# An S5 layer in split fp32 on one core: high and low parts a step apart, table work spread, one chain for two rows of x, and all residuals added from SBUF

## The chip, the cores and the metric

One core of a Trainium2 chip runs the whole program. Its engines are named as in the profile: PE (TensorE, matmuls; PEld is its weight load), DVE (VectorE), ACT (ScalarE), POOL (GpSimd) and SP (SyncE); SP and POOL also issue DMAs, each in its own order, one queue per engine. The metric is the device time of one execution in microseconds; a lower one is better. Times of a run are given as the median of several executions.

## The reference

The model is a trunk of interleaved mixers, but with depth 1 only layer 0 runs, which is the S5 state-space layer. x has 1024 positions of 2048 features:

```
h    = RMSNorm(x) * pre_norm
u, z = split(h @ w_in)                       # 2048 x 4096
A    = exp((a_re + i a_im) dt), dt = exp(log_dt)          # 128 groups x 64 states
B    = (A - 1)/(a_re + i a_im) * (b_re + i b_im)          # 16 channels to 64 states, each group
st_t = A st_(t-1) + B u_t                    # over 1024 positions
y    = Re(C st) + d_skip * u
g    = gelu(y)
y    = g * sigmoid(g @ w_glu + b_glu) * silu(z)           # 2048 x 2048
out  = x + RMSNorm(y @ w_out) * post_norm                 # 2048 x 2048
```

## The kernel before

**Split products.** Every large product is made of three: each fp32 operand is split into a high part (a copy rounded to the matmul's format, by ACT) and a low part (the rest, operand minus high part, by DVE), and PE adds high x high, high x low and low x high into one PSUM bank. `split_piece` does this for a weight piece of 128x512: an ACT copy (L171) and a DVE subtraction (L176). Where a weight term is itself a difference that no earlier step has stored, a DVE subtraction (L168) comes first. `split` (L833, L834) does the same for activations.

**Positions.** Row s of the eight "rows" of x holds positions 8k+s; a half is four such rows. x's rows are loaded, squared (`sq_x`: ACT L268 for even column blocks, DVE L270 for odd ones), turned into a reciprocal root (`rstd_x`, `_rsqrt`) and a scaled identity (`diag_x`), and transposed by PE (`trans_x`, L297) into the activations `hT`. At the start rows 0 and 1 have one chain together, rows 2 and 3 one each.

**Stage 1, the input projection.** 32 column tiles of `w_in` (16 for u, 16 for z) in two halves, in `units`; each inner turn is one block of 128 rows (L911, L913, L915). A weight piece covers four turns and is loaded (`load_piece`, on SP) and split a few pieces ahead (`begin_piece`; LA pieces for the load, SA for the split). Background work is handed out by `advance`, once per turn and half; such a unit is called a slot. First runs the generator `prep`, one `yield` per slot: it transposes tables on PE (L493), negates and copies (DVE L503, L504, ACT L495), multiplies the B coefficients (DVE L516, L517, L519) and stores the tables to DRAM from POOL. Then `plan` puts S5's work into slots: 32 heads (four groups each), one every TICK = 26 slots, each with a list of steps at fixed offsets (`s5_steps`: loads, coefficients, rotation, a scan on DVE L685, products L641, L667, L699, L700, gelu). Offsets ahead of the start are clamped to start + 1. Sums and differences of weight blocks for the next stages (`weight_sums`, L739) come every TSET = 19 slots: loads, and six and eight slots later the subtractions.

**Stages 2 and 3, GLU and output product.** Both are one level of Strassen's scheme in Winograd's form: seven products of half-size blocks each (`GLU_ORDER`, `OUT_ORDER`; L1229). Each product takes 16 steps (two column halves of eight), a step being one weight piece and its twelve matmuls. After each step `step()` hands out other work from five queues under a budget of four DVE operations: `front` (PSUM evacuation), `back` (next product's activations, by `ahead`: load, and two items later use), `mid` (gates, sums), `gains` (multiplying by post_norm, L1126) and `side` (weight sums left over, later the finished rows). The last product of the output stage is finished one row at a time with all its weights in SBUF (L1246 to L1248).

**The residual.** During stage 1, 23 DMAs on SP copy x (256 KB each) straight from DRAM into the output. When rows are done, `out_scale_tile` scales a 128x512 tile on ACT (L1165) and POOL's queue adds it onto the output in DRAM (L1162). Nine of the 32 tiles go the other way: x is loaded to SBUF (L1172), DVE scales and adds (L1178), SP stores plainly (L1179).

**Order.** Instructions are issued in the program's order on each engine and each queue; a tile's buffer is reused when its last reader is done. Nothing is reordered by a scheduler. Three buffers hold high weight parts in stage 1, four later; seven and later nine hold raw weights and low parts.

## Time and profile before

| | |
|---|---|
| median of 3 runs | 1516.75 us (1516.06 to 1519.03) |
| the profiled execution | 1519.02 us, its span 1517.2 us |
| PE busy | 1474.1 us, 97% of the span, 7288 matmuls |
| DVE busy | 1101.6 us, 73%, 2158 instructions |
| ACT busy | 666.3 us, 44% |
| POOL busy | 406.8 us, 27% |
| DMA | 332.01 MB, mean 219 GB/s |
| granted PE clock | 0.994 of full over the execution |

A row of the profile has the line of the kernel, the engine, the operation, the tile written and the tiles read, then busy time; in a timeline the first two numbers are start and length in us, and what stands in square brackets is the engine's idle time before the instruction and what ended it. PE is given as busy almost throughout, but a matmul's modelled length (some 0.39 us for 512 columns) is longer than the distance from one start to the next, so counts of starts in a window tell more than busy time.

### The profile page before, as it was taken

How to read it: one execution, taken by the hardware profiler on the slowest of the kernel's cores; microseconds unless marked ns; L12 is line 12 of the kernel's file. 1: busy time of each engine (PE TensorE's matmuls, PEld its weight loads, DVE VectorE, ACT ScalarE, POOL GpSimd, SP SyncE). 2: the span in 40 equal slices, each digit the busy share in tenths (PEclk: the TensorE clock that was granted, in tenths of full speed). 3: DMA queues.
4: the chain of work that ended last, by engine and by line, in shares of the span. 5: the costliest groups of instructions: out<-in, count | busy, mean ns of one | idle time of the engine just before them, and what ended most of it. 6: DMA issues, size and time to landing. Idle time of an engine off the chain costs nothing.

```text
span 1517.2 us, 22596 instructions
## 1 busy us (share of the span) xinstructions
PE 1474.1 (97%) x7288; PEld 1195.8 (79%) x7288; DVE 1101.6 (73%) x2158; ACT 666.3 (44%) x1223; POOL 406.8 (27%) x730
## 2 busy tenths in 40 slices
PE   6989999999999999999999999999999999998996
PEld 6867887878888888888888888788888878886774
DVE  7774888888878889888876346765788763577756
ACT  6642344444545454454543343432344353333553
POOL 5912243433434333423332102100112310000031
PEclk9999999999999999999999999999999999999998
DMA  7376767768677767765564449995889984675587
GB/s 275 97 231 170 227 171 231 211 200 237 183 225 207 237 173 237 201 186 170 149 195 132 156 160 335 358 311 164 293 314 358 370 297 160 182 222 190 160 209 170
DMA packets 252183, 332.01 MB, mean 219 GB/s; under 512 B 31280, under 2 KB 150112, under 8 KB 250912
## 3 DMA queue, kind: packets, MB, share of 16 engines
q1 hardware_dynamic: 217536, 251.14, 53.0%
q0 software_dynamic: 34528, 79.43, 17.2%
q8 instruction: 57, 0.93, 0.3%
q14 instruction: 62, 0.51, 0.1%
HBM read 244.54 MB, written 91.82 MB: 222 GB/s over the span
## 4 chain that ended last, share of the span: by engine, by line
PE 82%; DMA 7%; DVE 5%; issue 2%; ACT 2%; SPq 1%; POOL 0%; DVEq 0%; ACTq 0%; POOLq 0%
PE ps_d L911 15%; PE ps_d L1229 15%; PE ps_d L913 15%; PE ps_d L915 15%; PE ps_s L1229 14%; PE ps_s L667 2%; PE ps_s L700 2%; PE ps_s L699 2%; DMA w_raw<-in_s_w_out_dram 2%; DMA w_raw<-glu_T 1%; DVE w_raw L176 1%; ACT w_hi L171 1%; PE ps_s L641 1%; DMA gl<-g_d 1%; PE ps_s L297 1%
## 5 line engine op out<-in xcount | busy, mean ns | idle before, releaser
L171 ACT ACTIVATE w_hi<-w_raw 128x512 fp32r<-128x512 f32 x320 | 200.6, 630 | 487.6 <-PE ps_d L913 254.0
L176 DVE TENSOR_TENSOR w_raw<-w_raw,w_hi 128x512 fp32r<-128x512 f32 x320 | 222.3, 697 | 220.7 <-ACT w_hi L171 214.9
L911 PE MATMUL ps_d<-act,w_hi 128*128 128x512 f32 x1024 | 335.7, 404 | 0.0
L913 PE MATMUL ps_d<-act,w_hi 128*128 128x512 f32 x1024 | 322.8, 391 | 0.0
L915 PE MATMUL ps_d<-act,w_raw 128*128 128x512 f32 x1024 | 321.9, 390 | 0.0
L915 PEld LDWEIGHTS ps_d<-act,w_raw 128*128 128x128 f32 x1024 | 192.8, 188 | 41.3
L913 PEld LDWEIGHTS ps_d<-act,w_hi 128*128 128x128 f32 x1024 | 192.9, 188 | 40.8 <-DVE act L304 0.7
L911 PEld LDWEIGHTS ps_d<-act,w_hi 128*128 128x128 f32 x1024 | 185.2, 189 | 43.5 <-issue 10.2
L1229 PE MATMUL ps_d<-w_hi,act 128*128 128x512 f32 x448 | 140.7, 392 | 0.6 <-ACT w_hi L171 0.6
L1229 PE MATMUL ps_d<-act,w_hi 128*128 128x512 f32 x448 | 139.5, 392 | 0.0
L1229 PE MATMUL ps_s<-act,w_hi 128*128 128x512 f32 x448 | 139.3, 392 | 0.0
L1229 PE MATMUL ps_s<-w_hi,act 128*128 128x512 f32 x384 | 121.7, 395 | 3.2 <-ACT w_hi L171 3.2
L717 POOL DMA_DIRECT2D g_d<-gel_g x128 | 77.6, 614 | 144.8 <-DVE gel_g L715 133.8
L654 POOL DMA_DIRECT2D T<-hp_d x128 | 76.8, 618 | 110.4 <-issue 69.7
L1229 PEld LDWEIGHTS ps_d<-w_hi,act 128*128 128x128 f32 x448 | 84.1, 188 | 19.9 <-ACT w_hi L171 1.5
L1229 PEld LDWEIGHTS ps_s<-act,w_hi 128*128 128x128 f32 x448 | 84.1, 188 | 19.1
L1229 PEld LDWEIGHTS ps_d<-act,w_hi 128*128 128x128 f32 x448 | 84.0, 188 | 19.2 <-DVE ev L858 0.3
L833 ACT ACTIVATE act<-act 128x512 fp32r<-128x512 f32 x112 | 69.8, 626 | 57.2 <-DVE act L1019 29.8
L739 DVE TENSOR_TENSOR wsum<-wsum 128x256 f32<-128x256 f32 x156 | 65.9, 422 | 37.7 <-DMA wsum<-in_s_w_glu_dram 21.0
L1229 PE MATMUL ps_d<-w_raw,act 128*128 128x512 f32 x224 | 88.7, 396 | 1.1 <-DVE w_raw L176 1.0
L1162 POOL DMA_DIRECT2D out_dram<-act x23 | 19.8, 924 | 259.9 <-ACT act L1165 259.9
L1229 PE MATMUL ps_d<-act,w_raw 128*128 128x512 f32 x224 | 88.2, 394 | 1.3 <-DVE w_raw L176 1.3
(289 smaller groups left out, 2372.0 us busy)
## 6 DMA issues: line engine op xcount, KB each, us to landing
w_raw<-in_s_w_in_dram SPq DMA_DIRECT2D x136, 256.0 KB
w_raw<-in_s_w_out_dram SPq DMA_DIRECT2D x80, 256.0 KB
act<-g_d SPq DMA_DIRECT2D x72, 256.0 KB
wsum<-in_s_w_glu_dram SPq DMA_DIRECT2D x128, 128.0 KB
glu_T<-wsum POOLq DMA_DIRECT2D x128, 128.0 KB, 5.2
w_raw<-glu_T SPq DMA_DIRECT2D x64, 256.0 KB
w_raw<-in_s_w_glu_dram SPq DMA_DIRECT2D x48, 256.0 KB
u_d<-ev SPq DMA_DIRECT2D x128, 64.0 KB
```

What stands on the lines that cost most here:

```text
L171: act.activation(h, lf, AF.Copy)
L176: v.tensor_tensor(l, lf, h.bitcast(F32), op=OP.subtract)
L654: nc.gpsimd.dma_start(t[:, g], bass.AP(tensor=a.tensor, offset=a.offset + 16, ap=[[16, 8], [256, 16], [1, 128]]))
L667: pe.matmul(pv[64 * par:64 * par + 64, hh, i], lhsT=st["W1"][:, 2 * i + par, hh], rhs=st["U"][:, 2 * i + par], start=True, stop=True, tile ...
L699: pe.matmul(py[:, g], lhsT=st["T"][:, g], rhs=st["U"][:, g], start=True, stop=False)
L717: nc.gpsimd.dma_start(g_d[blk][4 * o + j].rearrange("c s k -> s c k"), g[:, NK * j:NK * j + NK])
L739: v.tensor_tensor(b[into], b[x], b[y], op=OP.subtract)
L833: act.activation(h, r, AF.Copy)
L911: pe.matmul(o, lhsT=wh[:, js], rhs=xh, start=kt == 0, stop=False)
L913: pe.matmul(o, lhsT=wh[:, js], rhs=xl, start=False, stop=False)
L915: pe.matmul(o, lhsT=wl[:, js], rhs=xh, start=False, stop=kt == KT - 1)
L1229: pe.matmul(pp[j], lhsT=st_, rhs=mv, start=start and i == 0, stop=stop and i == 2)
```

## The change

Seven edits, in the order of the code:

1. The reciprocal root has one operation less (two products merged with scalings); in the last rows it has two less, and a factor of -1/16 that is put into the post_norm tiles makes up for it.
2. `split_piece` becomes `split_hi` and `split_lo`. In stage 1 the low part is emitted at the second of a piece's four turns instead of right behind the high part; in stages 2 and 3 one step later. `ahead` does the same for activations with a third call, `finish`.
3. At the start, rows 2 and 3 of x share one chain; the squares are dealt out anew between ACT and DVE. Rows 4 to 7 are all loaded at the first weight piece.
4. `prep` yields more often: once more in each of four table groups, three times more in each of four coefficient groups, and three times less ahead of the second transposes.
5. S5's pool is opened 13 slots ahead of the start, so that nothing has to be clamped.
6. TICK 26 to 25, TSET 19 to 18, and the weight differences nine and eleven slots behind their loads.
7. The copies of x to the output go. Every tile's residual is loaded to SBUF (six items ahead in the first half of the rows finished), added by DVE, and stored by SP.

```diff
@@ _rsqrt
-    v.tensor_tensor(t, r, r, op=OP.mult)
+    v.scalar_tensor_tensor(t, r, -0.5 * k, r, op0=OP.mult, op1=OP.mult)
     v.tensor_tensor(t, t, var, op=OP.mult)
-    v.tensor_scalar(t, t, -0.5 * k, 1.5 * k, op0=OP.mult, op1=OP.add)
-    v.tensor_tensor(dst, r, t, op=OP.mult)
+    v.scalar_tensor_tensor(dst, t, 1.5 * k, r, op0=OP.add, op1=OP.mult)
@@ split_piece
-    def split_piece(i):
+    def split_hi(i):
...
         act.activation(h, lf, AF.Copy)
+        split_of[i] = l, lf, h
+
+    def split_lo(i):
+        if i not in split_of:
+            return
+        l, lf, h = split_of.pop(i)
...
         v.tensor_tensor(l, lf, h.bitcast(F32), op=OP.subtract)
@@ prep
             v.tensor_scalar(o2[0:64, c], pv[64:128], -1.0, None, op0=OP.mult)
+            yield
             v.tensor_scalar(o2[64:128, c], pv[0:64], -1.0, None, op0=OP.mult)
             yield
...
                 v.tensor_tensor(t1, bsw[:, a, sl], frb, op=OP.mult)
+                yield
+                yield
                 v.tensor_tensor(t2, bsw[:, b, sl], fib, op=OP.mult)
+                yield
                 yield
                 v.tensor_tensor(bb[:, sl, o], t1, t2, op=op)
@@ plan
-    TICK, TSET = 26, 19
+    TICK, TSET = 25, 18
...
-    def residual(s, r, c):
-        nc.sync.dma_start(ok[s][r, c], xk[s][r, c])
     def plan(start):
+        at(start - 13, s5_open)
         at(start, s5_begin)
-        for i, a in enumerate(resid):
-            at(start + TICK * i + 23, residual, *a)
         for h in range(HB):
             for off, f, a in s5_steps(h):
-                at(max(start + 1, start + TICK * h + off), f, *a)
+                at(start + TICK * h + off, f, *a)
...
-            at(i + 6, first)
-            at(i + 8, second)
+            at(i + 9, first)
+            at(i + 11, second)
...
-    BG0, YA, YB = KT, 6, 7
+    BG0, YA, YB = KT, 6, 4
@@ begin_piece
-                split_piece(done[0])
+                split_hi(done[0])
+        if late:
+            finish_piece(i + SA[0] - 1)
         return hi_t.pop(i), lo_t.pop(i)
+
+    def finish_piece(i):
+        while lows[0] < min(i, done[0]):
+            lows[0] += 1
+            split_lo(lows[0])
@@ start
-    for s in (2, 3):
-        for c in range(NQ):
-            sq_x(s, c)
-        rstd_x(s, 1)
-        diag_x(s)
-        if s == 3:
-            split_piece(0)
-        for k in range(NE):
-            trans_x(0, k, first[k], (s,))
-    split_piece(1)
+    for s, c, sc in ((2, 2, 1), (2, 1, 0), (2, 3, 1), (3, 0, 1), (3, 1, 0), (3, 2, 1), (3, 3, 0)):
+        sq_x(s, c, bool(sc))
+    rstd_x(2, 2, lambda: split_hi(0))
+    diag_x(2)
+    diag_x(3)
+    split_lo(0)
+    for k in range(NE):
+        trans_x(0, k, first[k], (2, 3))
+    split_hi(1)
+    split_lo(1)
...
-    xload = {0: (4,), 1: (5,), 2: (6,), 3: (7,)} if KT == 16 else {0: (4, 5, 6, 7)}
+    xload = {0: (4, 5, 6, 7)}
...
+                if j == 1 and not late:
+                    finish_piece(done[0])
@@ ahead
             if i < n:
                 got[i] = load(i)
-            if i >= lag:
-                use(i - lag, got.pop(i - lag))
+            if 0 <= i - lag < n:
+                use(i - lag, got[i - lag])
+            if i > lag:
+                finish(i - lag - 1, got.pop(i - lag - 1))
@@ output
-    def out_store(h, s, n, t):
-        nc.gpsimd.dma_start(ok[4 * (1 - h) + s][:, n * 512:(n + 1) * 512], t, accum_op=OP.add)
-    def out_scale_tile(h, s, n):
-        act.activation(Y[h, s, n], Y[h, s, n], AF.Copy, scale=yr[h][:, s:s + 1])
-        out_store(h, s, n, Y[h, s, n])
+    def load_res(h, s, n, pool):
+        xr[h, s, n] = fetch(xk[4 * (1 - h) + s][:, n * 512:(n + 1) * 512], pool)
+    def out_tile(h, s, n):
+        t = xr.pop((h, s, n))
+        v.scalar_tensor_tensor(t, Y[h, s, n], yr[h][:, s:s + 1], t, op0=OP.mult, op1=OP.add)
+        nc.sync.dma_start(ok[4 * (1 - h) + s][:, n * 512:(n + 1) * 512], t)
...
+    def second_half(i):
+        s, n = divmod(i, 4)
         while any(g == (1, s, n) for g in gained):
             gain_next()
-        if s < 3 and n:
-            load_res(1 + s, n)
-        out_scale_tile(1, s, n)
+        out_tile(1, s, n)
+        if i + XA < 16:
+            load_res(1, *divmod(i + XA, 4), act2)
+    XA = 6
...
+        if (kind, m) == ("out", 4):
+            side.extend([lambda: None] * 8)
+            side.extend(lambda i=i: load_res(1, *divmod(i, 4), act2) for i in range(XA))
         if (kind, m) == ("out", 3):
-            side.extend([lambda: None] * 6)
+            side.extend([lambda: None] * 2)
             side.append(lambda: out_scale(1))
-            side.extend(lambda i=i: second_half(*divmod(i, 4)) for i in range(16))
+            side.extend((1, lambda i=i: second_half(i)) for i in range(16))
+            for i in range(16):
+                side.append(lambda i=i: load_res(0, *divmod(i, 4), act2 if i < 12 else actp))
@@ last rows
-        _rsqrt(nc, fin, yr[0][:, s:s + 1], yv, "yl", 1, 0.125)
+        act.activation(r, va, AF.Sqrt)
+        v.reciprocal(r, r)
+        v.scalar_tensor_tensor(t, r, va, r, op0=OP.mult, op1=OP.mult)
+        v.scalar_tensor_tensor(yr[0][:, s:s + 1], t, -3.0, r, op0=OP.add, op1=OP.mult)
         for n in range(4):
-            out_last(s, n)
+            out_tile(0, s, n)
```

More of the change, by code (lines that the diff above doesn't have):

```diff
@@ L276, in rstd_x @@
         v.tensor_scalar(var[:, c], var[:, c], 1.0 / D, EPS, op0=OP.mult, op1=OP.add)
-        _rsqrt(nc, sm, rstd[:, c], var[:, c], "xr%d" % n, n)
+        _rsqrt(nc, sm, rstd[:, c], var[:, c], "xr%d" % s0, n, meanwhile=meanwhile)
     def diag_x(s):
@@ L761, in at @@
         thunks.setdefault(slot, []).append((f, a))
-    ok = out.rearrange("(k s) d -> s k d", s=NS)
-    resid = [(s, slice(32 * i, 32 * i + 32), slice(0, D)) for s in range(5) for i in range(4)] \
-        + [(s, slice(0, 128), slice(0, 512)) for s in range(5, NS)]
-    def residual(s, r, c):
-        nc.sync.dma_start(ok[s][r, c], xk[s][r, c])
     def plan(start):
+        at(start - 13, s5_open)
         at(start, s5_begin)
-        for i, a in enumerate(resid):
-            at(start + TICK * i + 23, residual, *a)
         for h in range(HB):
             for off, f, a in s5_steps(h):
-                at(max(start + 1, start + TICK * h + off), f, *a)
+                at(start + TICK * h + off, f, *a)
         i = start + 20
@@ L863, in s5_trunk_kernel @@
             sq_x(s, c)
+    sq_x(2, 0, True)
     rstd_x(0, 2)
@@ L946, in s5_trunk_kernel @@
                 first_of_g.append((kt, h, l))
+    ok = out.rearrange("(k s) d -> s k d", s=NS)
     front, mid, back, gains, side = deque(), deque(), deque(), deque(), deque()
@@ L964, in step, with ahead @@
                 n -= 1
-    def ahead(n, load, use, lag=2, queue=None, cost=1):
-        queue = back if queue is None else queue
+    def ahead(n, load, use, finish, lag=2, cost=1):
         got = {}
@@ L972, in item @@
                 got[i] = load(i)
-            if i >= lag:
-                use(i - lag, got.pop(i - lag))
-        for i in range(n + lag):
-            queue.append((cost if i >= lag else 0, lambda i=i: item(i)))
+            if 0 <= i - lag < n:
+                use(i - lag, got[i - lag])
+            if i > lag:
+                finish(i - lag - 1, got.pop(i - lag - 1))
+        for i in range(n + lag + 1):
+            back.append((cost if i >= lag else 0, lambda i=i: item(i)))
     def store(dst, t):
@@ L1015, in use @@
                 store(gs_d["S2"][kt], c)
-                raw = [c]
+                raw[:] = [c]
             elif raw:
@@ L1019, in use, with finish @@
                 v.tensor_tensor(a, a, b, op=OP.subtract)
-                raw = [a]
-            split(h, l, *raw)
+                raw[:] = [a]
+            act.activation(h, raw[0] if raw else l.bitcast(F32), AF.Copy)
+        def finish(kt, t):
+            h, l, raw = t
+            v.tensor_tensor(l, raw[0] if raw else l.bitcast(F32), h.bitcast(F32), op=OP.subtract)
             S[kind, m][kt] = h, l
-        ahead(KH, get, use, cost={("glu", "S2"): 3, ("glu", "S3"): 2, ("glu", "S4"): 2}.get((kind, term), 1))
+        ahead(KH, get, use, finish, cost={("glu", "S2"): 3, ("glu", "S3"): 2, ("glu", "S4"): 2}.get((kind, term), 1))
     R = {name: {} for name in ("X", "C11", "W", "C12", "C22")}
@@ L1188, in load_gain, with scale_gain @@
             pgain.append(g)
-    def second_half(s, n):
+    def scale_gain(n):
+        act.activation(pgain[n], pgain[n], AF.Copy, scale=-0.0625)
+    def second_half(i):
+        s, n = divmod(i, 4)
         while any(g == (1, s, n) for g in gained):
             gain_next()
-        if s < 3 and n:
-            load_res(1 + s, n)
-        out_scale_tile(1, s, n)
+        out_tile(1, s, n)
+        if i + XA < 16:
+            load_res(1, *divmod(i + XA, 4), act2)
+    XA = 6
     side.extend([lambda: None] * 20)
@@ L1206, in s5_trunk_kernel @@
             load_gain()
+        if (kind, m) == ("out", 6):
+            side.extend(lambda n=n: scale_gain(n) for n in range(4))
+        if (kind, m) == ("out", 4):
+            side.extend([lambda: None] * 8)
+            side.extend(lambda i=i: load_res(1, *divmod(i, 4), act2) for i in range(XA))
         if (kind, m) == ("out", 3):
-            side.extend([lambda: None] * 6)
+            side.extend([lambda: None] * 2)
             side.append(lambda: out_scale(1))
-            side.extend(lambda i=i: second_half(*divmod(i, 4)) for i in range(16))
+            side.extend((1, lambda i=i: second_half(i)) for i in range(16))
+            for i in range(16):
+                side.append(lambda i=i: load_res(0, *divmod(i, 4), act2 if i < 12 else actp))
         for nb in range(2):
@@ L1220, in s5_trunk_kernel @@
                     load_piece(last + kt, True)
-                    split_piece(last + kt - 3)
+                    split_hi(last + kt - 3)
+                    split_lo(last + kt - 4)
                 for j in range(4):
@@ L1236, in s5_trunk_kernel @@
     ws = []
+    yv = fin.tile([128, 4], F32, name="yv0")
     for s in range(4):
@@ L1240, in s5_trunk_kernel @@
             if s == 0:
+                for j in range(max(kt, 1), min(kt + 5, KH)):
+                    split_hi(last + j)
                 for j in range(kt, min(kt + 4, KH)):
-                    split_piece(last + j)
+                    split_lo(last + j)
                 ws.append((hi_t.pop(last + kt), lo_t.pop(last + kt)))
```

38 lines of the change are left out of this document (16 added, 22 removed).

## The prediction, made before the changed kernel had run

> **What bounds the kernel now.** I read the page's totals first, then who PE waited for, then busy time stage by stage, and last the instructions in order of time around each stage where PE loses time.
>
> ```profile
> span 1517.2 us, 22596 instructions
> PE 1474.1 (97%) x7288; PEld 1195.8 (79%) x7288; DVE 1101.6 (73%) x2158; ACT 666.3 (44%) x1223; POOL 406.8 (27%) x730
> ...
> PE ps_s L493 <- DVE tabA L519: 5.8, 2, 3.8
> PE ps_s L641 <- issue: 4.1, 2, 2.5
> ```
>
> PE sets the time, so an edit is worth only what PE's gaps shrink by, plus what changes ahead of its first product and behind its last. The change removes no big matmul. The two longest waits behind the startup (total, times, longest) name two places: the table transposes (L493) and the first S5 heads (L641). Busy time hides part of the loss, so I count matmuls per window (columns: length, PE, PEld, DVE, ACT, POOL busy with counts, clock, DMA share, GB/s):
>
> ```profile
> 96.00:100.00 4.00, 2.16 (x10) 1.46 (x8) 3.93 (x5) 0.63 (x1) 1.64 (x1) 1.00 0.72 221
> 100.00:104.00 4.00, 2.00 (x7) 1.83 (x8) 3.93 (x6) 0.87 (x1) 0.00 (x0) 0.71 1.02 308
> 104.00:108.00 4.00, 2.07 (x10) 1.49 (x10) 3.97 (x6) 1.23 (x2) 0.03 (x1) 0.86 0.54 158
> 108.00:112.00 4.00, 4.00 (x16) 3.29 (x15) 0.42 (x2) 1.31 (x2) 1.13 (x1) 0.57 0.56 217
> ...
> 120.00:160.00 40.00, 37.52 (x189) 30.04 (x187) 21.41 (x46) 11.54 (x26) 7.29 (x13) 1.00 0.59 165
> ...
> 400.00:560.00 160.00, 159.99 (x882) 129.95 (x881) 133.39 (x290) 75.57 (x142) 62.79 (x108) 1.00 0.71 206
> ...
> 1317.00:1361.00 44.00, 44.00 (x193) 36.04 (x193) 32.89 (x52) 15.60 (x30) 0.00 (x0) 1.00 0.74 232
> 1361.00:1417.00 56.00, 51.80 (x211) 39.95 (x210) 38.84 (x62) 21.13 (x45) 0.00 (x0) 0.97 0.54 172
> 1457.00:1481.00 24.00, 23.14 (x100) 18.35 (x99) 11.71 (x19) 13.14 (x26) 6.12 (x8) 1.00 0.88 212
> ```
>
> Undisturbed, PE starts 193 products in 44 us, 0.228 us each. In 1361 to 1417 that would be 246; 211 ran: 35 x 0.228 = **8.0 us** lost. In 1457 to 1481 5 are missing, **1.1 us**. The S5 stage (400 to 560) loses nothing.
>
> **The change, part by part.**
>
> *Startup.* Rows three and four of x get one chain instead of two.
>
> ```profile
> 10.04 0.69 DVE L270 SCALAR_TENSOR_TENSOR ev<-act 128x512 f32<-128x512 f32 x1 [0.70 <-DMA act<-in_x_dram]
> 12.00:13.00 1.00, 0.19 (x1) 0.19 (x2) 0.90 (x7) 0.78 (x3) 0.00 (x0) 1.00 1.06 410
> 17.00 0.69 DVE L270 SCALAR_TENSOR_TENSOR ev<-act 128x512 f32<-128x512 f32 x1
> 19.39 0.29 DVE L281 TENSOR_SCALAR ev<-ident,rstd 128x128 f32<-128x128 f32 x1
> 21.31 0.47 PE L911 MATMUL ps_d<-act,w_hi 128*128 128x512 f32 x1
> ...
> 28.85 0.89 PE ps_s L297 x8
> ```
>
> The eighth of sixteen x tiles is there at 10.0; eight more (2.1 MB) at about 0.4 MB per us are there at 15.3. Now the last square runs at 17.0 because DVE does the third row's chain first; after, it runs at 15.3. From there to the scaled identity the old chain takes 2.4 us (17.0 to 19.39); the new one has one step less and one identity more: first transposes at about 17.9. But there are two rows of them, not one: seven column blocks in two passes each, 28 instructions of 0.11 us (0.89/8), 3.1 us, so the first product starts near 21.0 instead of 21.3. I take **-0.3** (between -1 and +0.7, if data comes later). The three x loads that move ahead of the weight pieces delay pieces needed only two steps later: nothing.
>
> *The tables.* DVE is full (3.93 of 4 us) from 96 to 108 while PE waits for it. The 13 extra turns give 13 slots of three products, 13 x 0.68 = 8.8 us more cover before the transposes of `bb`, with the same DVE work. The wait is 5.8 us, but the four windows hold 43 matmuls, 16 of them transposes: 27 x 0.228 + 16 x 0.11 = 7.9 of 16 us, so 8.1 are lost. I leave 0.6 (one or two more weight splits fall between DVE's table work): **-7.5** (from -8.1 to -4). The clock column, 0.71, 0.86 and 0.57, is why the loss exceeds the wait.
> The Trainium skill (TensorE: Matmul & The Clock Gate, Part 1) says that PE falls to half clock after an idle window of about 3.4 us and needs as long a busy one to recover; by that rule the lost time is the 8.1 of the count, and by the waits alone 5.8, which would make the sum 2.3 us smaller. The trace agrees in that the 2.48 us wait below stands in a stretch (120 to 160) whose granted clock stays at 1.00.
>
> *The first heads.* S5's pool opens 13 slots ahead and head 0's coefficient loads go out 11 slots earlier instead of being clamped behind the start.
>
> ```profile
> 121.32 0.48 DVE L545 MEMSET S<- 128x512 f32 x1 [1.68 <-DMA tab_d<-st]
> ...
> 133.20 0.69 DVE L599 TENSOR_TENSOR rotcb<-pw,bb 128x512 f32<-128x512 f32 x1 [8.12 <-DMA bb<-bb_d]
> 139.36 0.76 DVE L592 TENSOR_TENSOR Q<-Q,otmp 128x576 f32<-128x576 f32 x1
> 140.22 0.43 PE L641 MATMUL ps_s<-Q,tab 128*32 128x128 f32 x8 [2.48 <-issue]
> ...
> 240.60 0.89 DVE L739 TENSOR_TENSOR wsum<-wsum 128x256 f32<-128x256 f32 x2 [5.97 <-DMA wsum<-in_s_w_glu_dram]
> 247.23 0.42 PE L641 MATMUL ps_s<-Q,tab 128*32 128x128 f32 x8 [1.63 <-issue]
> ```
>
> PE reaches the build at 140.22 - 2.48 + 8.8 - 7.5 = 139.0, and even loads that land as late as now give Q at 140.1. SP may stand at the new load until the table store lands (121.3, when the old pool's space comes free); behind it are weight pieces needed two steps (10 us) later. **-2.0** (-2.5 to -1). The wait at 247 follows DVE's 6 us wait for a weight-sum load; the subtraction moves three slots back and 23 copies leave SP and the DMA engines: **-1.0** (-1.6 to 0).
>
> *Ticks of 25 and 18 slots.* PE's work is the same; only DVE's room shrinks.
>
> ```profile
> 286.00 1.02 PE ps_s L667 x16
> 307.33 1.02 PE ps_s L667 x16
> ```
>
> A head takes 21.33 us, of which DVE is busy 133.39/160 = 83%, 17.8 us. A slot less (3 x 0.228) makes it 20.65, 86%. I charge **+1** for new waits (0 to +5). More than that is unlikely, since half of the 416 us in which DVE is not busy goes to one wait, for a high part that itself waits for PE, and the low part now comes two turns of the inner loop later:
>
> ```profile
> L176 DVE TENSOR_TENSOR w_raw<-w_raw,w_hi 128x512 fp32r<-128x512 f32 x320 | 222.3, 697 | 220.7 <-ACT w_hi L171 214.9
> ```
>
> *High and low a step apart.* In the out products with L168, each weight piece goes DVE (subtract), ACT (high), DVE (low), and DVE stands still for ACT each time:
>
> ```profile
> DVE w_raw L176 <- ACT w_hi L171: 14.4, 17, 1.4
> ACT w_hi L171 <- DVE act L168: 22.6, 12, 2.6
> ...
> 1375.40 0.68 DVE L168 TENSOR_TENSOR act<-w_raw,act 128x512 f32<-128x512 f32 x1
> 1378.68 0.68 DVE L168 TENSOR_TENSOR act<-w_raw,act 128x512 f32<-128x512 f32 x1
> ```
>
> A piece takes 3.28 us where PE's twelve products take 12 x 0.228 = 2.74, so PE catches up with the split and waits. Without the 14.4 us of standing DVE's 38.8 busy us fit into 56. Of 8.0 I take **-7.0** (-8 to -1).
>
> *Residuals.* 23 copies of x to the output and 23 adding stores on POOL go; 23 loads, 23 plain stores on SP and 23 DVE operations of 0.7 us come (the row of three in the tail, 2.08), where ACT did as many.
>
> ```profile
> q0 software_dynamic: 2304, 4.20, 47.1%
> q1 hardware_dynamic: 3899, 7.09, 40.9%
> ...
> 1464.32 0.63 ACT L171 ACTIVATE w_hi<-w_raw 128x512 fp32r<-128x512 f32 x1 [6.46 <-DMA w_raw<-in_s_w_out_dram]
> ```
>
> From 1435 to 1490 (queue, packets, MB, share) a MB of adding store costs 11.2% of the engines, a plain one 5.8%: a load and a store cost as much as the one they replace, but the first six loads move ahead of this stretch. The weight load that came late (1464) also goes out a step earlier, since the low part takes its buffer later: **-0.8** of 1.1 there, and **-1.5** in the last product, whose pieces come late behind the same traffic (its 96 products go from 1480.51 to 1504.78, 24.3 us for 21.9, so 2.4 are lost; 0 to -2.4, since DVE's own work of the second product's sums also falls there). SP now waits for DVE ahead of each store with weight loads queued behind; they are five pieces (13.7 us) ahead.
> The Trainium skill (Trainium Kernel Development and Optimization, Key Constraints) says that DMAs of all queues share the same 16 engines, so that another queue saves issue time only. By that alone these two terms would be nought and the sum 2.3 us smaller; the two shares above say that adding itself costs engine time.
>
> *Tail.*
>
> ```profile
> 1480.51 0.39 PE L1246 MATMUL ps_s<-act 128*128 128x512 f32 x1
> ...
> 1504.55 0.39 PE L1248 MATMUL ps_s<-act 128*128 128x512 f32 x1
> 1507.91 2.08 DVE L1178 SCALAR_TENSOR_TENSOR act<-act,yr,act 128x512 f32<-128x512 f32 x3
> 1508.93 0.85 POOL L1162 DMA_DIRECT2D out_dram<-act  x1 [4.58 <-ACT act L1165]
> 1510.02 0.33 SPq L1179 DMA_DIRECT2D out_dram<-act  x1
> ```
>
> From the last product to the three operations at 1507.91 some ten steps take 3.1 us; two of the small ones go, about 0.4, and a fourth operation of 0.7 comes: DVE ends 0.3 later. The adding store of 1508.93 no longer shares the engines with the last plain one; its excess is 0.262 MB x (11.2 - 5.8)% of 55 us per MB = 0.8 us. Between +0.3 (all of it beside other transfers) and -1.3 (twice the excess); I take **-0.5**.
>
> **Sum:** -0.3 -7.5 -2.0 -1.0 +1.0 -7.0 -0.8 -1.5 -0.5 = -19.6. The profiled execution took 1519.02 us (1.8 around its span), the median is 1516.75, so 1499.4 by the one and 1497.2 by the other; since the runs to come give a median, I predict **1497**.
>
> **The rivals.**
> *Everything is hidden* (chance 0.15): every term at its better end, -1 -8.1 -2.5 -1.6 -8 -1.1 -2.4 -1.3 = -26: 1491. For it: most waits have the one cause that the change takes away. Against: DMA is full in places.
> *The split stage keeps its wait* (0.12): if DVE is short of throughput there, and not held up by the order of its work, the 7 us stay: 1504. For it: a piece's four DVE operations of 0.69 us fill PE's 2.74. Against: DVE is 69% busy (38.84 of 56).
> *SP's stores hold up the last weight loads* (0.12): SP is in order, and a late subtraction, the full engines of the third product (256 KB each of weight, activation, residual in, residual out per 2.74 us is 380 GB/s, near the 410 seen above) let loads slip; the late load now costs 6.46 us of ACT's wait, so some 7 of the gain go: 1504.
> *S5 turns DVE-bound: slower* (0.08). The place is the 32 heads; if DVE with its waits needs more than 20.65 us, each head costs the difference. The gain of 20.6 without the charged 1, and the 3.0 below, are eaten at 20.65 + 23.6/32 = 21.4 us, that is if none of the 3.5 us in which DVE now stands idle in a head can be used, and it decides from there. At 21.6 it is 32 x 0.95 = 30 us on 1496: 1526. For it: denser weight sums ask for the same engine. Against: from 400 to 560 PE was busy 159.99 of 160.
>
> **How the numbers follow.** Forecast 0.53, rivals as given. This kernel's runs tell a difference from about 0.2%, 3 us. Faster holds the forecast, the first three rivals, less a little for mishaps in several at once: 0.88; same 0.05; slower 0.07. The range 1488 to 1507 holds the forecast, its bounds and the first three rivals, with 3 us at either end for the spread of the runs (1516.06 to 1519.03 now); the slower one is left out.
>
> **What would show it.** L493 without a wait on L519 and a clock of 1.00 from 96 to 112; L641 at 140 and 247 without a wait; the full 246 products in 56 us where L168 runs and no DVE wait on L171 there; no late ACT wait for the last product's weights; no PE wait between 250 and 960. Wrong would be new waits of PE on Q, S or the high parts in the S5 stage, or DVE full from 1405 to 1480 with SP waiting for it.

## The result

The changed kernel takes 1482.12 us (median of 4 runs, 1481.76 to 1482.89) beside 1516.73 us (1516.06 to 1519.03) for the kernel before: a ratio of 0.977, 95% interval 0.9753 to 0.9787, 34.6 us less. The forecast was 1497 with a range of 1488 to 1507: the sign was right, the gain was 15 us larger, and the time lies below the range. The profiled execution took 1482.26 us, 36.8 us less than the one before, with a span of 1480.4; the one before is the slowest of its four, so what is read from the two traces adds up to 2.2 us more than the medians differ by.

From the page after, totals, PE's clock in 40 slices, and the queue of POOL (packets, MB, share of the 16 DMA engines):

```profile
span 1480.4 us, 22613 instructions
PE 1455.2 (98%) x7288; PEld 1193.8 (81%) x7288; DVE 1108.5 (75%) x2151; ACT 653.4 (44%) x1205; POOL 386.6 (26%) x707
...
PEclk9999999999999999999999999999999999999999
...
q0 software_dynamic: 31216, 73.40, 15.1%
```

PE's waits in the profile after, whom it waited for, in us in total, times, longest:

```profile
PE ps_s L444 <- DMA gtmp<-in_s_b_glu_dram: 6.3, 1, 6.3
PE ps_s L305 <- DMA act<-in_x_dram: 5.6, 1, 5.6
PE ps_s L1253 <- DVE w_raw L184: 2.7, 2, 2.2
PE ps_s L655 <- PE ps_d L929: 1.0, 1, 1.0
PE ps_s L655 <- DVE Q L606: 0.8, 1, 0.8
```

The first two belong to the startup. Neither the tables' wait (transposes, now L501) nor one for a high part is left. Busy time by window after, with the columns of the windows in the prediction (length, PE, PEld, DVE, ACT, POOL with counts, clock, DMA share, GB/s):

```profile
100.00:104.00 4.00, 4.00 (x19) 3.30 (x19) 3.96 (x6) 0.63 (x1) 0.00 (x0) 1.00 1.02 304
104.00:108.00 4.00, 4.00 (x24) 3.39 (x23) 3.93 (x6) 0.74 (x1) 0.06 (x1) 1.00 0.64 178
...
1297.00:1341.00 44.00, 44.00 (x196) 36.45 (x195) 36.43 (x59) 16.74 (x32) 0.00 (x0) 1.00 0.75 241
1341.00:1397.00 56.00, 56.00 (x249) 46.39 (x248) 43.91 (x75) 28.09 (x58) 0.00 (x0) 1.00 0.63 205
1433.00:1457.00 24.00, 24.00 (x107) 19.88 (x106) 20.79 (x36) 11.17 (x28) 0.00 (x0) 1.00 0.67 230
```

The split stage runs 249 matmuls in 56 us instead of 211, at full clock. The surprise stands one row above it: a stage of 44 us that had no wait before does 196 instead of 193. To see where the time went, I number the 5760 products of 512 columns in order of time (both kernels have the same) and compare the start of the k-th. Worked out from both traces (differences are taken before rounding):

```
      k      before   after   ahead by   what lies between this row and the one above
      0        21.3    20.9      0.4     startup
    240        96.6    95.7      0.9
    360       134.9   124.7     10.1     the tables
   3000       855.4   841.9     13.5     first heads, S5 stage
   5160      1355.3  1335.5     19.8     GLU and output products up to the split stage
   5400      1418.5  1389.9     28.6     the split stage
   5664      1480.5  1449.7     30.8     up to the last product
   5759      1504.5  1471.3     33.2     the last product
 span end    1517.2  1480.4     36.8     the tail
```

The 6.2 us between k = 3000 and 5160 have no term in the prediction, and the tail's 3.5 had one of 0.5. Between k = 3000 and 5664, the next product starts 228 to 245 ns later (median 233) at 1406 of the 2664 products of the kernel before, and 227 ns later (mean 226.7) at the others, but for 39 that wait longer; the 1406 take together 8.3 us over 226.7. After, 31 are slow in this way.

### The profile page after: what moved, and what is told of

Same layout as the page of the kernel before. It is cut to its first block, busy times and chain, and to the rows that moved or that the text cites. A ratio compares the mean times of both kernels' runs of the same rounds, so it can differ in the third digit from the quotient of the medians.

```text
span 1480.4 us, 22613 instructions
## 1 busy us (share of the span) xinstructions
PE 1455.2 (98%) x7288; PEld 1193.8 (81%) x7288; DVE 1108.5 (75%) x2151; ACT 653.4 (44%) x1205; POOL 386.6 (26%) x707
## 4 chain that ended last, share of the span: by engine, by line
PE 90%; DMA 4%; DVE 2%; issue 2%; SPq 1%; ACT 1%; POOL 0%; DVEq 0%; ACTq 0%; POOLq 0%
PE ps_d L1253 19%; PE ps_s L1253 18%; PE ps_d L925 15%; PE ps_d L927 15%; PE ps_d L929 14%; PE ps_s L681 2%; PE ps_s L714 2%; PE ps_s L713 2%; PE ps_s L305 1%; DMA act<-in_x_dram 1%; DMA act<-g_d 1%; PE ps_s L655 1%; DVE act L1190 1%; DMA zl<-z_d 0%; PE ps_s L307 0%
## 5 line engine op out<-in xcount | busy, mean ns | idle before, releaser
L1253 PEld LDWEIGHTS ps_d<-act,w_hi 128*128 128x128 f32 x448 | 84.0, 188 | 17.7 <-DVE ev L871 0.3
L1253 PE MATMUL ps_s<-act,w_raw 128*128 128x512 f32 x224 | 87.5, 391 | 2.9 <-DVE w_raw L184 2.7
L754 POOL DMA_DIRECT2D glu_T<-wsum x128 | 71.8, 582 | 63.8 <-DVE wsum L753 61.4
L1253 PEld LDWEIGHTS ps_s<-w_hi,act 128*128 128x128 f32 x384 | 72.1, 188 | 14.9
```

Source lines behind the costliest of these rows:

```text
L754: nc.gpsimd.dma_start(t_d[kind, t][kt][:, cols], b[into])
L1253: pe.matmul(pp[j], lhsT=st_, rhs=mv, start=start and i == 0, stop=stop and i == 2)
```

## The experiments

Times are medians; the kernel before is the one measured on the same chip.

### High and low parts together again in the Strassen stages

*w_joined*, the weights alone:

```diff
                 split_hi(done[0])
+                if late:
+                    finish_piece(done[0])
-        if late:
-            finish_piece(i + SA[0] - 1)
```

> The changed kernel, but from the first Strassen product on each weight piece's low part is issued right behind its high part again; the activations stay apart. My theory: in the kernel before, the weight splits let DVE stand for ACT, parts came just in time, and PE then ran products at 0.231 to 0.236 us instead of 0.2267 (about 6.3 us from the first to the split stage), and lost about 8 us in the split stage where L168 runs before. Then this run loses most of both: about 1482 + 6 + 8 = 1496, with 193 products in 44 us before the split stage. Rival 1, the activations' splits did it: the pace stays at 194 in 44 us and only the split stage is lost, about 1490. Rival 2, neither did (the old residual traffic or the buffers did): 1490 as well, and the run with both joined shows the same.

*a_joined*, the activations alone: `use` ends with `finish(kt, t)`, and the third call of `ahead` is gone.

> The changed kernel, but each activation tile's low part is issued right behind its high part again; the weights stay apart. My theory (the weights set the pace): no change, 1482 to 1484. Rival 1 (the activations set it): the 6.3 us of pace between the first Strassen product and the split stage come back, about 1488, with 191 to 193 products in 44 us there.

*wa_joined*, both edits:

> The changed kernel with both the weights' and the activations' low parts right behind the high ones in the Strassen stages. My theory: pace as in the kernel before (0.2293 us mean) and the split stage's 8 us lost: 1496 to 1498. If the pace has another cause (residual traffic, buffers), it stays at 0.2267 up to the split stage and the time is about 1490.

Measured: 1498.72, 1485.47 and 1503.50 us (before 1518.04; ratios 0.9872, 0.9783, 0.9903 with intervals of 0.003 to 0.0035 on either side). Weights carry most of it, and the two together cost 21 us. But my theory of the pace fell: wa_joined runs 620 matmuls in 140 us where the changed kernel has 619, and only 140 of its 2664 products are slow (228 to 245 ns). Its loss is waits, distances of more than 245 ns: over 227 ns a product they come to 8.7 us in the split stage, 8.2 behind it and 1.7 in the last product, whose own pieces stay apart in this run; another 2.8 us are lost ahead of k = 3000, where its code is that of the changed kernel.

*b_apart*, the kernel before with this one part: `split_piece` in two, `ahead` with `finish`, in the Strassen stages and the last product only.

```diff
-                split_piece(done[0])
+                split_hi(done[0])
+                if not late:
+                    finish_piece(done[0])
+        if late:
+            finish_piece(i + SA[0] - 1)
```

> The kernel before with one part of the change alone: high and low parts a step apart in the Strassen stages and the last product, all else as it was. My theory: it gains the 6.3 us of pace, the split stage's 8 and some of the late load: 1516.7 - 15 to 16.5 = 1500 to 1502, with 194 products per 44 us before the split stage. Rival (the pace comes from another part of the change): only the split stage, about 1508.

Measured: 1511.89 us (ratio 0.9959, 0.9945 to 0.9974), 6.1 us less. The split stage is clean, as its window shows:

```profile
1361.30:1416.40 55.10, 55.10 (x241) 45.07 (x240) 44.21 (x71) 25.04 (x54) 0.00 (x0) 1.00 0.61 200
```

but 1362 of 2664 products are still slow. So the pace belongs to another part of the change.

### Where the last pools lie

The slow products stand in a pattern. Here are 96 in a row, from the 4728th on, in the output products; # is a distance of 228 to 245 ns to the next start, a point is 227:

```
before      ####################.....#####.#####............##.#################............................
b_apart     ##################.#####........................####################............................
wa_joined   ................................................................................................
after       ................................................................................................
```

They come back every 48 products: four weight pieces, and there are four buffers for high weight parts, the fourth in a pool of its own (`wp2`). In the built program `wp2` and `act2` lie behind the small tiles of `fin`. At its end `fin` has nine places of 32 bytes for the tail's sums and roots before and ten after (two buffers of `yp` less; `yv0` and second buffers of `yl_r` and `yl_t` more). With them `act2` starts at byte 189152 of each partition before, 32 past a multiple of 64, and at 189184 after, a multiple of 64. Sorting the 2664 distances of the kernel before by operand: of the 1120 where an operand of the product or of the next one lies 32 bytes past, 1038 are slow; of the 1544 others 368, and 335 of these come within eight products behind one that is off.

*b_shift32* and *a_shift32* add one tile of 32 bytes at the head of `fin`, to the kernel before and to the changed one, and nothing else:

```diff
             fin = ctx.enter_context(tc.tile_pool(name="fin", bufs=1))
+            v.memset(fin.tile([128, 1], F32, name="shift"), 0.0)
```

> The kernel before, with one more small tile (32 bytes of each partition, set to zero once) at the head of the last pools, and nothing else. It moves the Strassen stages' second activation pool and second weight pool from 32 bytes beyond a multiple of 64 to a multiple of 64, where the changed kernel has them (its tail holds one small tile more and another fewer). New theory, since with high and low apart alone half of the products before the split stage (1056 of 2160) still stood more than 228 ns behind the one before them, in a pattern of 48 products, four weight buffers, while with both joined in the changed kernel 34 of 2160 did: PE takes 231 to 236 ns instead of 227 where an operand starts 32 bytes off. Then all products before the split stage come 227 ns apart, 6.3 us there and some 1.6 behind it are gained: about 8 us below the kernel before, 1509, with the split stage's waits left (a little of the gain may go into them). Rival (the pace belongs to another part of the change): no difference.

> The changed kernel with the same small tile, which moves its two pools to 32 bytes beyond a multiple of 64. By the placement theory half the products of the Strassen stages take 231 to 236 ns again: 7 to 8 us slower, 1490. By the rival (another part of the change sets the pace): 1482, pace 0.2267.

Measured: 1513.67 us (before 1517.30; ratio 0.997, 0.9955 to 0.9984) and 1489.41 us (ratio 0.981, 0.979 to 0.983). 140 us in the middle of the Strassen stages, first the kernel before, then with the tile:

```profile
1040.00:1180.00 140.00, 140.00 (x611) 114.40 (x610) 110.09 (x185) 55.12 (x91) 24.86 (x47) 1.00 0.84 296
```

```profile
1040.00:1180.00 140.00, 140.00 (x620) 115.91 (x619) 111.71 (x188) 55.06 (x92) 25.82 (x48) 1.00 0.85 300
```

and the changed kernel, then with the tile:

```profile
1025.00:1165.00 140.00, 140.00 (x619) 115.99 (x618) 113.30 (x189) 55.47 (x92) 27.18 (x51) 1.00 0.88 310
```

```profile
1025.00:1165.00 140.00, 140.00 (x611) 114.46 (x610) 111.18 (x185) 54.21 (x90) 24.39 (x46) 1.00 0.87 299
```

The count goes both ways with nothing but 32 bytes; slow products go from 1406 to 71 and from 31 to 1304. In the changed kernel that is worth about 7 us. In the kernel before only 3.6 arrive: its profiled execution takes 3.6 us longer from k = 240 to 3000, where the placement is the same as before (with the same code there, b_apart takes 757.8 us for this stretch and b_apart_shift 763.1), and its waits in the split stage and the last product grow by 1.3. The Trainium skill (SBUF — State Buffer, Operand start alignment) asks only that an operand start at a multiple of its element size, and says that this is about legality and that its runs timed nothing; both placements satisfy that, and the rows above give the time.

*b_apart_shift*: both single parts on the kernel before.

> The kernel before with two parts alone: high and low a step apart in the Strassen stages and the last product, and the 32-byte tile that puts the two pools at a multiple of 64. If the two add up (8 us of the split stage, 8 of placement, some waits of the last product left): 1517 - 14 to 16 = 1501 to 1503, with all products before and in the split stage 227 ns apart. If one hides what the other gives: 1507 to 1509.

Measured: 1503.37 us (before 1516.50; ratio 0.9909, 0.9877 to 0.994), 13 us less, where the two alone gave 6.1 and 3.6. Its products from k = 3000 to 5664 are all but 31 at 227 ns, and the split stage loses nothing. What is left behind k = 3000 is the tail and the last product, which loses 6.0 us to its own late parts, while ACT waits 7.3 us for weight loads; the changed kernel loses none there.

### The residuals

*res_old*: the changed kernel with copies, ACT's scaling and adding stores as before.

```diff
+        for i, a in enumerate(resid):
+            at(start + TICK * i + 23, residual, *a)
...
-        out_tile(1, s, n)
-        if i + XA < 16:
-            load_res(1, *divmod(i + XA, 4), act2)
+        if s < 3 and n:
+            load_res(0, 1 + s, n, act2)
+        out_scale_tile(1, s, n)
...
-            out_tile(0, s, n)
+            (out_tile if (0, s, n) in xr else out_scale_tile)(0, s, n)
```

> The changed kernel with the old residuals: 23 copies of x to the output during the S5 stage, and in the last two products and the tail 23 of the 32 output tiles scaled on ACT and added to the output by adding stores. By the prediction it loses 0.8 (late load), 1.5 (last product), 0.5 (tail) and about 0.5 (copies): 1485.5. By the two traces, where 33.2 - 28.9 us were gained between the middle of the third product and the last product and 3.5 behind it, up to 8: 1490, with 3.5 of it behind the last product.

Measured: 1486.73 us (before 1517.30), 4 to 4.6 more than the changed kernel's 1482.69 and 1482.12. In the profiled execution, the fastest of the four (1484.72), the last product starts its last matmul at 1470.5, 0.8 earlier than in the changed kernel: up to the last product the copies and adding stores cost nothing that shows. In the last product it loses 1.0 us (22.5 us instead of 21.6); there DVE waits 4.6 us for high parts from ACT, which scales tiles again, and 0.3 in the changed kernel. From the last start to the end of the span it takes 12.4 us instead of 9.1. The changed kernel's tail:

```profile
1471.31 0.39 PE L1275 MATMUL ps_s<-act 128*128 128x512 f32 x1
...
1474.28 0.16 DVE L1298 SCALAR_TENSOR_TENSOR yr<-yl_t,yl_r 128x1 f32<-128x1 f32 x1
1474.48 2.74 DVE L1190 SCALAR_TENSOR_TENSOR act<-act,yr 128x512 f32<-128x512 f32 x4
```

DVE is done at 1477.22 and the span ends 3.2 us later. In the kernel before the adding store is issued at 1508.93 and the span ends at 1517.2. The page of its output tile gives the adding stores' landing (us from issue, least, median, most):

```profile
L1162 POOL DMA_DIRECT2D out_dram<-act x23: 843/852/1646, 1435.7 to 1508.9; - x23
...
DMA to landing us min/median/max: 4.1/7.8/10.1
```

*res_tail* leaves the old way to four tiles, one in each of the last rows:

```diff
+    resid = [(s, slice(0, 128), slice(0, 512)) for s in range(4, NS)]
...
-            out_tile(0, s, n)
+            (out_tile if (0, s, n) in xr else out_scale_tile)(0, s, n)
```

> The changed kernel, but the first column block of each of the last four row blocks takes the old way: x copied to the output during the S5 stage, scaled on ACT, added by an adding store from POOL's queue; the other 28 stay. If the tail's gain is the time that the last adding store takes to land (7.4 us from its issue's end to the end before, 3.2 from the last operation's end after), this run ends 12.4 us behind the start of the last product instead of 9.1: 1485.5, as with all old residuals. If it is the sum of the traffic of all adding stores: 1483 to 1484.

Measured: 1485.30 us (before 1516.50). The profiled execution ends 11.4 us behind the last product's last start, 2.3 more than the changed kernel, with DVE a little sooner (three operations, until 1481.63) and this as its last store:

```profile
1479.55 2.08 DVE L1197 SCALAR_TENSOR_TENSOR act<-act,yr 128x512 f32<-128x512 f32 x3
1480.56 0.86 POOL L1202 DMA_DIRECT2D out_dram<-act  x1 [4.58 <-ACT act L1201]
```

The span ends at 1487.9, 7.4 us behind the start of that issue. So four adding stores cost most of what 23 did, and it is the last one that counts. (The rest of this execution's 7.5 us lies mostly at the first heads, 4.5 us between k = 480 and 840.)

The number came out as the first theory had it, but landing is only a part of the reason. In the kernel before, the last adding store lands at 1513.80, 4.9 us behind the start of its issue, the last packet of the plain store beside it ends at 1513.87, and SP has seen both by 1514.6. What the program then still waits for is POOL: its closing DRAIN, an instruction that stands behind the program's last one, runs from the last issue, 1508.91, for 7.52 us to 1516.43 (times of one: least, median, most in ns):

```profile
L1290 POOLq DRAIN  x3: 46/98/7522, 1508.9 to 1516.9; - x3
```

In the changed kernel POOL issues nothing behind 1208 us, and its long DRAIN is over there:

```profile
L1322 POOLq DRAIN  x3: 46/98/6131, 1208.2 to 1480.2; - x3
```

In res_tail the last adding store lands at 1485.35 and the DRAIN ends at 1487.16; in res_old at 1479.57 and 1482.16. From DVE's last result to the last packet of the output it is 3.9 us before, 4.0 in res_old, 3.9 in res_tail and 1.7 in the changed kernel. So of the tail, some 2.2 us are stores that land sooner and 1.8 the DRAIN that ended later still; DVE, which ends 0.5 later behind the last product, takes that back. What the DRAIN waits for isn't shown.

*joined_res_old*: res_old with the two edits of wa_joined.

> The changed kernel with high and low together again in the Strassen stages and the residuals as before. Together alone cost 21 us, of which 8.7 in the split stage, 8.2 in the third product's time behind it, where the kernel before loses only 1.4. My theory: those 8.2 come from the residuals' operations, which stand on DVE in the changed kernel and on ACT before, in front of the low parts; then this run has the split stage's loss but 1 to 2 us there, plus 3.3 for the tail: 1503.5 - 7 + 3.3 = 1499 to 1500. Rival (the loss there has nothing to do with the residuals): 1503.5 + 3.3 = 1507.

Measured: 1499.56 us (before 1516.50; ratio 0.9881, 0.9861 to 0.9901), as my theory had it. Behind the split stage wa_joined lost 8.2 us, this run 0.2. The windows behind the split stage, wa_joined first:

```profile
1402.00:1470.00 68.00, 63.70 (x265) 49.96 (x264) 50.18 (x86) 27.91 (x59) 0.00 (x0) 0.97 0.66 210
```

```profile
1402.00:1462.00 60.00, 60.00 (x266) 49.34 (x265) 40.03 (x70) 37.96 (x78) 13.74 (x16) 1.00 0.85 221
```

The waits in these windows say how. In wa_joined SP stands at the residuals' stores, which wait for DVE, and ACT waits for the weight loads that are queued behind them on SP:

```profile
SPq L1190 <- DVE act L1189: 35.8, 15, 10.7
```

```profile
ACT w_hi L173 <- DMA w_raw<-in_s_w_out_dram: 27.3, 8, 7.8
```

In joined_res_old ACT's wait for such loads is 8.2 us in 2 times. In the changed kernel SP stands 22.7 us at the stores and ACT 17.7 for loads, and PE loses nothing from it.

### The tables and the S5 stage

*prep_old* takes the 13 turns out again and puts YB back to 7:

```diff
             v.tensor_scalar(o2[0:64, c], pv[64:128], -1.0, None, op0=OP.mult)
-            yield
...
                 v.tensor_tensor(t1, bsw[:, a, sl], frb, op=OP.mult)
-                yield
-                yield
                 v.tensor_tensor(t2, bsw[:, b, sl], fib, op=OP.mult)
                 yield
-                yield
```

> The changed kernel with the tables' work closed up as before (the 13 turns taken out, 7 turns ahead of the transposes of bb instead of 4). By the prediction's reading it loses what the turns gave, 7.5 us (9.2 by the two traces): 1490 to 1491, with the wait for the tables and the half clock back between 96 and 112 us. If the low parts' later place did it instead: under 2 us, 1484.

*early_joined* puts the low parts of the input projection's pieces back behind the high ones:

```diff
                 split_hi(done[0])
+                if not late:
+                    finish_piece(done[0])
```

> The changed kernel with high and low parts of the input projection's weight pieces issued together again, the Strassen stages apart. The closed-up tables' work cost only 5 us of the 9.2 that were gained there, so the later low part should be worth the rest: 4 us lost, 1486, at the tables and the first heads. If the low part's place is worth nothing there: 1482.

Measured: 1487.63 us (before 1517.30) and 1487.00 us (1483.62 to 1490.70; before 1517.24). In prep_old the wait is back, without the half clock of the kernel before:

```profile
96.00:100.00 4.00, 2.59 (x15) 1.91 (x14) 3.97 (x6) 0.78 (x2) 0.00 (x0) 1.00 1.02 315
100.00:104.00 4.00, 1.48 (x9) 1.01 (x7) 3.93 (x5) 1.78 (x2) 0.00 (x0) 1.00 0.64 187
```

```profile
PE ps_s L501 <- DVE tabA L527: 4.2, 2, 2.8
```

It costs 5 to 5.5 us (4.5 at k = 480), not the 9.2 gained there. early_joined has no wait at the tables:

```profile
100.00:104.00 4.00, 4.00 (x19) 3.32 (x18) 3.96 (x6) 0.63 (x1) 0.00 (x0) 1.00 1.02 303
```

It loses 4.3 us in the median; its runs overlap those of after_again (1481.71 to 1485.48). The profiled execution, its slowest, is 2.4 us behind after_again at k = 480, the first heads, 6.1 at k = 3000, with a wait of PE for a scan of 1.9 us (L714 for L707) between, and 8.2 at k = 5160, though from the Strassen stages on its code is the same. So the turns remove the tables' wait, and the later low parts probably help the heads; how much is theirs isn't shown.

*ticks_old* (TICK 26, TSET 19) and *after_again*, the changed kernel on the same chip:

> The changed kernel with a head each 26 slots and a set of weight sums each 19, as before. The prediction charged 1 us for the shorter ones: 1481. By the traces (14.7 us ahead at the first heads, 13.5 at the end of the S5 stage) up to 1.2 us less than the changed kernel; if DVE's room makes no difference, the same 1482.

> The changed kernel as it is, beside the next three on one chip: 1482, with 227 ns between products and the 2.2 us wait of PE for a low part near 945 us.

Measured: 1483.42 (1481.52 to 1485.97) and 1482.69 us (1481.71 to 1485.48); at k = 3000 they stand at 842.6 and 842.5. The shorter ticks cost nothing and give nothing that can be told.

### The wait that is left

*a_gap* loads the weight sums of the Strassen stages one step sooner:

```diff
-        side.extend(tsets.popleft()(lambda: act2.tile([128, 512], F32, name="act2")[:, :256]))
-        side.extend([lambda: None] * 2)
+        ld, *rest = tsets.popleft()(lambda: act2.tile([128, 512], F32, name="act2")[:, :256])
+        side.extend((ld, lambda: None, *rest, lambda: None))
```

> The changed kernel, but each set of weight sums that is made during the Strassen stages is loaded two steps ahead of its first subtraction instead of one (an empty step moves from behind the set to between them). In the changed kernel DVE stands 3.9 us at such a subtraction for its load at 942 to 946 us, PE then waits for a low part behind it (2.2 us) and runs some products slower after it, 3.8 us over the pace between the first Strassen product and the split stage. If that load is the cause, most of it goes: 1479 (3 us less). If DVE is short of time there because of the three operations of the third product's sums, nothing: 1482.

Measured: 1480.91 us (1480.25 to 1482.03) beside 1482.69 for the changed kernel, 1.8 less, about 0.1%; the runs of the two overlap. DVE from 925 us on, the changed kernel (to 948) and this one (to 955):

```profile
DVE act L753 <- DMA act<-in_s_w_out_dram: 3.9, 1, 3.9
```

```profile
DVE act L1077 <- DMA zl<-z_d: 3.6, 1, 3.6
```

The load came in time, and DVE now stands at the next late one. PE's wait goes from 2.2 to 1.2 us. Of the expected 3 us 1.8 came, if that; the DMA share there is 0.92 to 0.99 in the changed kernel (942 to 952 us), so it may be that a load that is moved ahead pushes another back; that was not tried.

## Why the prediction was right, and where it was wrong

**Startup, -0.3:** 0.4 by the two traces. But the changed kernel's first product starts at 20.9 us in this trace and at 21.3 in after_again's, as in the kernel before, so a gain of this size can't be told.

**The tables, -7.5 (bounds -8.1 to -4):** 9.2 between k = 240 and 360. The cause was right: L501 waits for nothing, the clock stays at 1.00, and taking the turns out brings the wait back. The size was not: the 8.1 were counted from 96 to 112 only. prep_old accounts for some 5; its profile differs from the kernel before in that its longest wait is 2.8 us instead of 3.8 and that the clock stays full. The kernel before has two stretches of 3.41 us at half clock there, at 101.7 and 108.5; half of PE's busy time in them, some 3 us, is an estimate of what they cost. Which edit keeps prep_old's waits below those of the kernel before was not tried by itself.

**First heads, -3.0, and ticks, +1:** together 3.4 between k = 360 and 3000, forecast 2.0. The charge for the ticks was not needed (ticks_old). PE has no wait for Q beyond 0.8 us, as forecast. By early_joined the low parts' later place probably belongs to this gain; the prediction had counted it on DVE's room only.

**The Strassen stages ahead of the split stage, no term:** 6.2 us, and 1.5 more of pace in the split stage and behind it, nearly half of the 17.2 us by which the traces' gain of 36.8 is above the sum of 19.6. This is the step that failed: "Undisturbed, PE starts 193 products in 44 us, 0.228 us each." I took the pace of a window without waits for PE's own. The window had no wait, but 87 of the 192 products that start in it were slow, by some 6 ns, by the place of their operands; their mean distance is 0.2293. In the input projection of the same trace every product that stands more than ten behind a smaller one is followed by the next after 226 or 227 ns; comparing the two would have shown that 0.228 was not the floor. The edit that removed it is the tail's exchange of small tiles, which the prediction read only for its operations.

**The split stage, -7.0 (-8 to -1):** 8.8, of which 0.7 are pace. The mechanism was right and alone enough (b_apart clears the stage). The 1 us that I left for rest was not there.

**Late load and last product, -2.3:** 4.7 between k = 5400 and 5759, 0.8 of it pace. The reason given, the traffic of the adding stores, sized by their 11.2% against 5.8% per MB, does not show: res_old, which has them, loses nothing at the late load (59.8 us from k = 5400 to 5664, as the changed kernel) and 1.0 us in the last product, where ACT waits 1.2 us for loads, less than the 2.3 of the changed kernel; late there are ACT's high parts. wa_joined loses 1.7 us in the last product and b_apart_shift, with parts apart, 6.0; what clears it in the changed kernel lies in edits that no run took out alone, the order and cost of the finished rows' work among them. This stays open.

**Tail, -0.5 (-1.3 to +0.3):** 3.5. Here too a step failed: "its excess is 0.262 MB x (11.2 - 5.8)% of 55 us per MB = 0.8 us". The adding store's share of the engines was taken for its delay. The direction was right, since the plain store beside it lands sooner without it, but that is worth some 2.2 us and not 0.8, and POOL's DRAIN behind its last issue, 1.8 us beyond the landing, was in no term. After, the last plain store's landing and the end fit into 3.2 us behind DVE. res_tail shows the loss with four tiles.

**The rivals.** "SP's stores hold up the last weight loads" names a real mechanism: wa_joined has it, 8.2 us behind the split stage. With high and low apart its cover is long enough. This is a large part of why that edit gives 6 us alone and costs 21 when it is taken out: the residuals' new way needs it (with the old one, taking it out costs 12.8 us: joined_res_old against res_old). "S5 turns DVE-bound" did not happen: at 25 slots a head the S5 stage has no lasting wait, and 26 change nothing. "Everything is hidden", 1491, was the nearest; the time is below even that, since placement and POOL's DRAIN were in no bound.

From k = 3000 to the last start the kernel before takes 649.1 us, b_apart_shift 634.2 and the changed kernel 629.4. So parts apart and placement give 14.9 of the 19.7 us there; of the other 4.8, the last product makes 6.0, less 1.2 by which b_apart_shift is ahead of the changed kernel between k = 3000 and 5160.

## What to carry to other kernels

Before taking a pace without waits as the floor, compare it with the same instruction in another stage of the trace; a difference of 2% over thousands of products is worth more than most waits, and small tiles ahead of a pool can set it. The last transfer of a program costs not its bytes but the time from its issue to the end: its landing, and what the engine that issued it still does behind the issue (a DRAIN of 7.5 us here). So the engine that adds should have its last issue early; in these runs only taking all of them away was tried. Two edits that hide each other's waits are to be sized together: one alone showed 6 us here, its removal 21.

## What the runs showed of the hardware

**Placement.** In the Strassen stages a 128x128 by 128x512 fp32r product starts 227 ns behind the one before it when all operands lie at multiples of 64 bytes in SBUF, and mostly 229 to 236 ns when one of them or of the next product's lies 32 bytes past, and for up to eight products behind; a shift of 32 bytes turns it on and off. Why the ones behind are slow too isn't shown. Placement isn't the only thing that goes with slow products: in the input projection all operands of these products lie at multiples of 64, and yet 579 of the 2865 that another one follows at once are slow before, and 591 after. All of them stand second to tenth behind a smaller product, of the tables, the transposes or S5; why isn't shown either.

**The clock after short waits.** In a_joined a gap of 2.48 us between two products, from 932.4, is followed by products 426 ns apart. In the changed kernel a gap of 2.58 us at 944.3 is followed by none, and its clock stays full. So the length of one wait did not decide, and both are under the idle window of about 3.4 us that the Trainium skill (TensorE: Matmul & The Clock Gate, Part 1) gives for half clock. The traces show what does: in each of the 17 the granted clock changes only on a grid of steps 3.41 us wide, counted from its first rise at 15.7 to 18.7 us, and the idle time inside one step counts. a_joined's gap lies in one step, with PE busy for 1.32 us of it, and the next step is at half clock:

```profile
931.66:935.07 3.41, 1.32 (x7) 0.78 (x6) 2.68 (x5) 1.15 (x2) 1.08 (x2) 1.00 0.89 275
935.07:938.49 3.42, 3.42 (x9) 2.68 (x10) 2.69 (x5) 1.67 (x4) 1.08 (x2) 0.50 1.01 379
```

The changed kernel's gap is shared by two steps:

```profile
942.25:945.66 3.41, 2.41 (x11) 1.67 (x9) 0.00 (x0) 0.83 (x2) 0.47 (x1) 1.00 0.87 224
945.66:949.07 3.41, 2.22 (x10) 1.83 (x11) 3.27 (x7) 0.63 (x1) 1.19 (x3) 1.00 1.01 387
```

The 17 traces have 22 changes from full to half clock ahead of the last product's end. Each comes behind a step in which PE stood 1.4 to 3.4 us, by the modelled ends of its matmuls, and no step at full clock with more than 1.9 us is without one; from 1.4 to 1.9 us both are seen. So less than a whole idle step was enough here.

**Adding stores.** They took 4.1 to 10.1 us from issue to landing in the kernel before, 4.6 to 6.4 where only four were left. POOL's DRAIN behind its last issue took 6.1 us in the changed kernel, 6.6 in res_tail, 7.5 in the kernel before and 7.6 in res_old.
